# Hybrid Mamba-2 / RWKV-7 decoder layer on one Trainium2 core: four edits in the recurrent stage

## The chip, the cores and the metric

One Trainium2 chip, one of its eight cores. The metric is the device time of one execution of the program in microseconds (us). All arithmetic is on 32-bit floats. The median of three runs of the kernel before is 2946.23 us (2942.55 to 2946.69).

## The reference, cut to what matters

The program is one decoder layer for a prompt of 1024 tokens and 8 samples of 8 tokens each. It has an input projection, a Mamba-2 branch, an RWKV-7 branch, a merge, an output projection and a convolutional gated feed-forward block. The change touches the RWKV-7 branch alone, whose core is this recurrence for 16 heads of 64 channels, with a normalisation of `kk` before it and a group norm after it:

```python
def _rwkv7_scan(r, decay, k, v, kk, a, S0):
    def step(S, inp):
        r_t, w_t, k_t, v_t, kk_t, a_t = inp
        sa = jnp.einsum('bhvk,bhk->bhv', S, -kk_t)
        S = (S * w_t[:, :, None, :] + sa[..., None] * (kk_t * a_t)[:, :, None, :]
             + v_t[..., None] * k_t[:, :, None, :])
        return S, jnp.einsum('bhvk,bhk->bhv', S, r_t)
...
    kk = kk / jnp.maximum(jnp.sqrt(jnp.sum(kk * kk, axis=-1, keepdims=True)), 1e-12)
...
    mu = jnp.mean(yb, axis=-1, keepdims=True)
    var = jnp.mean((yb - mu) ** 2, axis=-1, keepdims=True)
...
    yb = yb + jnp.sum(r4 * k4 * lp['rwkv_r_k'].astype(f32), axis=-1, keepdims=True) * v4
```

## The kernel before, in words

Activations stand as channels (partitions) by tokens; the 1088 tokens are cut into three token groups of 384, 384 and 320 columns, the last of which ends in the 64 sample tokens. Every large product takes three passes on TensorE: weights and activations are each split into a rounded part (`hi`) and the rest (`lo`), and `mm3` (lines 253 to 257) issues hi by hi, hi by rest and rest by hi. `run_dense` (line 259) runs through the weight tiles; these are called the dense matmuls here. After every second step of `mm3` it calls `bg.step()`, which advances the background work of the stage by one piece.

In the recurrent stage, which is the first third of the span, that background is RWKV-7. Heads go in 8 pairs `p`, token groups `tg` in 3, and each job (p, tg) passes four lanes of Python generators:

- `rw_prep` (line 486): gates, decays, the normalisation, and then the pairwise products of the tokens within a unit of 64 tokens (`pair`, line 571). These are 64x64-tile matmuls, 16 for four units, into two PSUM tiles of the pool with tag `t`; a VectorE multiplication with a mask empties each tile into `tt` (line 581).
- `rw_inv` (line 601): inverse of a triangular matrix per unit, by 32x32-tile matmuls (lines 703, 728, 744), and transposes (lines 638, 738).
- `rw_scan` (line 752): the recurrence over 4 or 6 units. A unit is a chain: matmul at line 771, `rh` on VectorE (773), matmul 775, two copies of one half each of `pc` into `sav`, one on VectorE (776) and one on ScalarE (777), matmul 779, new state on VectorE (781). There are 128 units. For samples the same two copies stand at lines 822 and 823, before the matmul at 827, and the new sample states are four products at line 845 (`quarters`, line 830): two head halves `hf` by two groups `b` of four samples. Half `hf` writes the PSUM partitions from 64 x `hf`.
- `rw_post` (line 865): group norm and gate.

Sums over the 64 channels of a head are `colsum` (line 404): the operand is split by `halves` (line 397) into `xh`, which ScalarE casts, and `xl`, the rest, which VectorE computes from `xh`; then two accumulating matmuls, first with `xh` (line 405), then with `xl` (line 406). `pst()` gives PSUM tiles of tag `t`, of which there are two.

The order of the instructions on each engine is not the order of the Python code: when the program has been recorded, a list scheduler with its own cost estimates places every instruction in its engine's queue as its operands become ready by these estimates. `small` (line 241) keeps a batch of small matmuls in order by queueing each behind the one before (`issue_after`), and can add one more dependency to the first of them (`wait`). The engines then run their queues in order, and wait wherever the real time is later than the estimate.

Of the kernel before, what the change touches and what calls it, by code (L numbers as in the profile page):

```python
# [12 lines left out]
AF = mybir.ActivationFunctionType  # L13
# [91 lines left out]
def tile_hybrid_step(  # L105
# [380 lines left out]
    def rw_prep(p, tg):  # L486
# [32 lines left out]
        S.activation(rn[:, :n], ps[:, :n], AF.Ln, bias=tiny)  # L519
# [46 lines left out]
        evacs = None  # L566
        for u in range(0, nu, 4):
# [10 lines left out]
            small([lambda j=j, c0=c0, hf=hf: pair(j, c0, hf) for j in range(m) for c0, hf in ((0, 1), (64, 0), (64, 1), (0, 0))], wait=evacs)  # L578
            msk = tms if (tg == 2 and u == 4) else tm
            for hf in range(2):  # L580
                evacs = V.tensor_tensor(  # L581
                    out=tt[:, u:u + m, hf::2, :], in0=pa[hf][:, :m].rearrange("p u (x c) -> p u x c", x=2),
                    in1=msk.rearrange("p (x c) -> p x c", x=2).unsqueeze(1).to_broadcast([128, m, 2, 64]), op=ALU.mult,
                ).ins
# [9 lines left out]
        V.tensor_tensor(out=bv[:, :n], in0=ps[:, :n], in1=vv[:, :n], op=ALU.mult)  # L594
# [6 lines left out]
    def rw_inv(p, tg):  # L601
# [108 lines left out]
        S.copy(re[:, :nu], p3)  # L710
        S.copy(rv[:, :nu], pvw)
# [5 lines left out]
        V.tensor_tensor(out=zc[:, :nu], in0=zc[:, :nu], in1=p3, op=ALU.add)  # L717
# [29 lines left out]
        for hf in range(2):  # L747
            r0 = 64 * hf
            V.tensor_copy(tt[r0:r0 + 32, :nu, hf, 32:64], p3[r0:r0 + 32])
        jobs[p, tg] = (ar, tt, sav, bkt, wend, rv)  # L750

    def rw_scan(p, tg):
# [14 lines left out]
        for u in range(npu):  # L767
# [9 lines left out]
            S.copy(sav[64:128, u, 1, :], pc[64:128, 1, 64:128])  # L777
# [17 lines left out]
        if tg == 2:  # L795
# [27 lines left out]
            S.copy(sav[64:128, u, 1, :], pc[64:128, 1, :])  # L823
# [6 lines left out]
            quarters = [(hf, b) for hf in range(2) for b in (0, 4)]  # L830
# [31 lines left out]
        S.copy(yt[:, :n], ps[:, :n])  # L862
        lanes["post"].add(rw_post(p, tg, yt), lambda: (p, tg) in bonus)

    def rw_post(p, tg, yt):
# [7 lines left out]
        S.activation(sq[:, :n], ps[:, :n], AF.Ln, bias=geps, scale=1.0 / 64.0)  # L873
# [8 lines left out]
        V.scalar_tensor_tensor(out=yt[:, :n], in0=yt[:, :n], scalar=pv("lnb", p), in1=ps[:, :n], op0=ALU.add, op1=ALU.mult)  # L882
# [823 lines left out]
```

## Time and profile before

| | |
|---|---|
| median of 3 runs | 2946.23 us |
| profiled execution | 2947.11 us, span 2945.2 us |
| PE busy over the span | 2834.9 us, 96% |
| DVE busy | 1878.3 us, 64% |
| ACT busy | 1365.3 us, 46% |
| mean granted TensorE clock | 0.988 |
| recurrent stage, matmuls of `rw_post` as its last | ends at about 1058 us |

PE is TensorE with its matmuls, PEld its weight loads, DVE VectorE, ACT ScalarE, POOL GpSimd. A matmul of fp32 operands shows as two instructions in the trace; one of the dense matmuls as one. The ends of matmuls are modelled, and a matmul that streams shows as some 0.31 to 0.34 us though the next begins 0.15 to 0.17 us after it: so the starts tell the pace, and idle time before a matmul is counted only from the modelled end of the one before.

### The profile page before, as it was taken

What the parts mean: (1) busy time and instruction counts of PE and PEld (TensorE: products, weight loads), DVE (VectorE), ACT (ScalarE), POOL (GpSimd) and SP (SyncE); (2) the same over time, 40 slices, a digit from 0 to 9 for tenths busy, and PEclk for the clock granted to TensorE, in tenths of its full rate; (3) what the DMA queues carried; (4) which work ended last, traced back from release to release, by engine and by line L of the source; (5) the groups of instructions that cost most, each with busy time, mean ns of one, the idle gap of its engine ahead of it and who ended that gap; (6) DMA issues with size and microseconds to landing.
All of it is one profiled execution on the core that took longest, in us unless ns stands there. A gap on an engine that the chain in (4) does not pass through costs nothing.

```text
span 2945.2 us, 57204 instructions
## 1 busy us (share of the span) xinstructions
PE 2834.9 (96%) x22822; PEld 2631.3 (89%) x22822; DVE 1878.3 (64%) x4097; ACT 1365.3 (46%) x3108; POOL 698.6 (24%) x890
## 2 busy tenths in 40 slices
PE   8999999999999999999999989999999999999998
PEld 7887888888878899888888889999999999999998
DVE  6788777787788755878787753544264444444435
ACT  6666556555566655666666641222242222222223
POOL 3112212122121133555554421542220000000001
PEclk9999999999999999999999999999999999999999
DMA  3111111111111232343434564432211111111112
GB/s 113 37 36 43 42 39 51 35 47 41 45 37 41 69 86 66 115 139 111 141 108 148 150 216 128 149 110 85 83 54 51 58 51 51 51 52 57 51 51 86
DMA packets 160355, 229.86 MB, mean 78 GB/s; under 512 B 20940, under 2 KB 124632, under 8 KB 160088
## 3 DMA queue, kind: packets, MB, share of 16 engines
q1 hardware_dynamic: 160088, 226.20, 24.3%
q8 instruction: 180, 2.95, 0.4%
q14 instruction: 87, 0.71, 0.1%
HBM read 177.89 MB, written 48.26 MB: 77 GB/s over the span
## 4 chain that ended last, share of the span: by engine, by line
PE 46%; DVE 8%; ACT 4%; DMA 2%; issue 2%; POOL 1%; DVEq 0%; SPq 0%; ACTq 0%; POOLq 0%
PE psd L255 14%; PE psd L256 14%; PE psd L257 14%; DVE acc L1050 2%; DVE sg L1137 1%; DVE wlo L238 1%; DMA ld<-ya_d 1%; DVE sg L1127 1%; DVE yj L1234 1%; PE py L1180 1%; DMA ld<-yb_d 1%; DVE yj L1237 1%; PE py L1217 1%; PE py L1181 0%; PE ph L1183 0%
## 5 line engine op out<-in xcount | busy, mean ns | idle before, releaser
L255 PE MATMUL psd<-act,whi 128*128 128x384 f32 (+1 forms) x4344 | 1474.5, 339 | 14.7 <-ACT act L215 5.2
L257 PE MATMUL psd<-act,wlo 128*128 128x384 f32 (+1 forms) x4344 | 1435.0, 330 | 4.7 <-DVE wlo L238 4.7
L256 PE MATMUL psd<-act,whi 128*128 128x384 f32 (+1 forms) x4344 | 1434.2, 330 | 4.3 <-DVE act L216 4.0
L255 PEld LDWEIGHTS psd<-act,whi 128*128 128x128 f32 x4344 | 822.6, 189 | 43.9 <-issue 19.3
L256 PEld LDWEIGHTS psd<-act,whi 128*128 128x128 f32 x4344 | 822.3, 189 | 22.1 <-issue 10.0
L257 PEld LDWEIGHTS psd<-act,wlo 128*128 128x128 f32 x4344 | 822.0, 189 | 7.9 <-DVE wlo L238 5.3
L237 ACT CAST whi<-wraw 128x512 fp32r<-128x512 f32 x382 | 226.6, 619 | 499.3 <-PE psd L256 491.4
L238 DVE TENSOR_TENSOR wlo<-wraw,whi 128x512 fp32r<-128x512 f32 x382 | 289.0, 780 | 260.7 <-ACT whi L237 255.0
L1442 DVE TENSOR_TENSOR macc<-macc,psd 128x384 f32<-128x384 f32 (+1 forms) x216 | 114.6, 531 | 74.2 <-PE psd L257 73.8
L1399 POOL COPY fpo<-fraw 128x2 f32<-128x2 f32 x22 | 9.5, 430 | 613.1 <-ACT fraw L1397 613.1
L1050 DVE SCALAR_TENSOR_TENSOR acc<-craw,par,acc 128x1112 f32<-128x1112 f32 x72 | 116.3, 1615 | 5.5 <-ACT acc L1047 4.8
L1138 POOL TENSOR_TENSOR csb<-csb,cc 128x512 f32<-128x512 f32 (+1 forms) x72 | 98.5, 1374 | 77.4 <-ACT dec L1136 64.0
L1394 ACT COPY fraw<-psd 128x384 f32<-128x384 f32 x44 | 21.1, 479 | 133.2 <-PE psd L257 133.2
L1304 POOL TENSOR_TENSOR ld<-ld,rw 128x384 f32<-128x384 f32 (+1 forms) x48 | 54.3, 1152 | 114.7 <-DMA ld<-ya_d 111.0
L1326 POOL TENSOR_TENSOR macc<-macc,gt 128x384 f32<-128x384 f32 (+1 forms) x48 | 53.6, 1118 | 107.1 <-DVE gt L1325 107.1
L546 POOL TENSOR_TENSOR ar<-rm,wq 128x384 f32<-128x384 f32 (+1 forms) x24 | 20.8, 867 | 237.9 <-ACT wq L524 221.1
L1325 DVE TENSOR_TENSOR gt<-psd,gt 128x384 f32<-128x384 f32 (+1 forms) x48 | 25.5, 533 | 77.9 <-PE psd L257 70.7
L713 POOL MEMSET tt<- 64x384 f32 (+1 forms) x48 | 18.1, 377 | 240.6 <-PE pst L697 239.1
L1137 DVE TENSOR_TENSOR sg<-sg,cbm 128x512 f32<-128x512 f32 (+1 forms) x72 | 73.5, 1045 | 0.6
L613 ACT COPY uc<-tt 32x192 f32<-32x192 f32 (+1 forms) x96 | 49.4, 515 | 52.5 <-DVE tt L581 51.3
L627 POOL TENSOR_TENSOR bk<-bk,wend 128x768 f32<-128x768 f32 (+1 forms) x24 | 34.2, 1426 | 140.7 <-PE pst L573 104.8
L779 PE MATMUL pc<-sav,bkt 128*128 128x128 f32 x256 | 59.3, 314 | 8.3 <-ACT sav L777 7.0
(405 smaller groups left out, 4360.8 us busy)
## 6 DMA issues: line engine op xcount, KB each, us to landing
wraw<-in_wts SPq DMA_DIRECT2D x191, 512.0 KB, 3.2
csb<-cs_d SPq DMA_DIRECT2D x64, 256.0 KB, 4.2
gt<-g_d SPq DMA_DIRECT2D x48, 192.0 KB, 2.3
zt<-z_d SPq DMA_DIRECT2D x32, 256.0 KB, 4.6
z_d<-ge SPq DMA_DIRECT2D x32, 192.0 KB, 1.9
ya_d<-yj SPq DMA_DIRECT2D x8, 768.0 KB, 4.4
ld<-ya_d SPq DMA_DIRECT2D x32, 192.0 KB, 3.2
g_d<-ge SPq DMA_DIRECT2D x28, 192.0 KB, 1.9
```

What stands on the lines that cost most here:

```text
L237: S.copy(hi[:, c:c + 512], t[:, c:c + 512])
L238: V.tensor_tensor(out=lo[:, c:c + 512], in0=t[:, c:c + 512], in1=hi[:, c:c + 512].bitcast(F32), op=ALU.subtract)
L255: PE.matmul(ps, a, act[:, 0, :n], start=first, stop=False)
L256: PE.matmul(ps, a, act[:, 1, :n], start=False, stop=False)
L257: PE.matmul(ps, b, act[:, 0, :n], start=False, stop=last)
L779: last = PE.matmul(pc[:, 2, :], bkt[:, u, :], sav[:, u, :, :].rearrange("p h c -> p (h c)"), start=True, stop=True).ins
L1050: V.scalar_tensor_tensor(out=acc, in0=raw[:, j:j + L], scalar=cw(j), in1=acc, op0=ALU.mult, op1=ALU.add)
L1137: V.tensor_tensor(out=sg[0:m, :, :m], in0=sg[0:m, :, :m], in1=cbm[0:m, :m].unsqueeze(1).to_broadcast([m, 4, m]), op=ALU.mult)
L1138: G.tensor_tensor(out=ec[:, :, :m], in0=ec[:, :, :m], in1=cx[:, q0:q0 + m].unsqueeze(1).to_broadcast([128, 4, m]), op=ALU.mult)
L1304: G.tensor_tensor(out=t[:, :n], in0=t[:, :n], in1=scales[k // 4, tg][:, :n], op=ALU.mult)
L1326: G.tensor_tensor(out=macc[m][tg][:, :n], in0=macc[m][tg][:, :n], in1=gt[:, :n], op=ALU.add)
L1442: V.tensor_tensor(out=x1[m][tg][:, :n], in0=x1[m][tg][:, :n], in1=ps[:, :n], op=ALU.add)
```

## The change

It makes four edits, all in the code of the recurrent stage.

1. `colsum` multiplies the rest first and the rounded part second.
2. `quarters` goes through the halves first and through the sample groups second, so that the two products that stand together write different halves of the PSUM partitions.
3. The second copy into `sav`, for units and for samples, moves from ScalarE to VectorE.
4. Instructions that empty a PSUM tile of tag `t` are noted in a list (`read`). The first matmul of each batch of pairwise products now depends on the last two of the list, the readers of both PSUM tiles that the batch takes over. Before, only a second batch had one such dependency, on the last mask multiplication.

```diff
+    readers = []
+
+    def read(ins):
+
+        readers.append(ins.ins)
+
-    def small(calls, behind=None, wait=None):
+    def small(calls, behind=None, wait=()):
...
-            if wait is not None:
-                tc.add_manual_dep(behind, wait.name, mybir.DependencyInfo(mybir.DependencyClass.Sync, mybir.DependencyReason.DATA), reason="small")
-                wait = None
+            for ins in wait:
+                tc.add_manual_dep(behind, ins.name, mybir.DependencyInfo(mybir.DependencyClass.Sync, mybir.DependencyReason.DATA), reason="small")
+            wait = ()
...
     def colsum(ps, m, parts_, n):
-        PE.matmul(ps[:, :n], m, parts_[0][:, :n], start=True, stop=False)
-        PE.matmul(ps[:, :n], m, parts_[1][:, :n], start=False, stop=True)
+        PE.matmul(ps[:, :n], m, parts_[1][:, :n], start=True, stop=False)
+        PE.matmul(ps[:, :n], m, parts_[0][:, :n], start=False, stop=True)
...
-        S.activation(sg[:, :n], ps[:, :n], AF.Exp, scale=-1.0, bias=nw0[:, p:p + 1])
+        read(S.activation(sg[:, :n], ps[:, :n], AF.Exp, scale=-1.0, bias=nw0[:, p:p + 1]))
...
-            small([lambda j=j, c0=c0, hf=hf: pair(j, c0, hf) for j in range(m) for c0, hf in ((0, 1), (64, 0), (64, 1), (0, 0))], wait=evacs)
+            small([lambda j=j, c0=c0, hf=hf: pair(j, c0, hf) for j in range(m) for c0, hf in ((0, 1), (64, 0), (64, 1), (0, 0))], wait=readers[-2:])
...
             V.tensor_copy(sav[0:64, u, 0, :], pc[0:64, 1, 0:64])
-            S.copy(sav[64:128, u, 1, :], pc[64:128, 1, 64:128])
+            V.tensor_copy(sav[64:128, u, 1, :], pc[64:128, 1, 64:128])
...
             V.tensor_copy(sav[0:64, u, 0, :], pc[0:64, 1, :])
-            S.copy(sav[64:128, u, 1, :], pc[64:128, 1, :])
+            V.tensor_copy(sav[64:128, u, 1, :], pc[64:128, 1, :])
...
-            quarters = [(hf, b) for hf in range(2) for b in (0, 4)]
+            quarters = [(hf, b) for b in (0, 4) for hf in range(2)]
```

`read(...)` is put around the other readers of `t` tiles in the same way. New lines shift the numbers: what is line 405, 573, 775, 776, 777, 779 before is 411, 578, 783, 784, 785, 787 after, and the dense 255, 256, 257 are 261, 262, 263.

Since the scheduler works the order out anew, much of the stage's order moves. Three places show how. The first is PE's queue in the first head pair, at a batch of pairwise products for four units (`pst<-ar_129,bk`, 16 matmuls). Before:

```order
L703 MATMUL pst<-vt,um 32x32 x24
L573 MATMUL pst<-ar_129,bk 64x128
L256 MATMUL psd<-act_340,whi 128x384
L257 MATMUL psd<-act_340,wlo 128x384
L255 MATMUL psd<-act_352,whi 128x384
L573 MATMUL pst<-ar_129,bk 64x128 x15
L256 MATMUL psd<-act_352,whi 128x384
L257 MATMUL psd<-act_352,wlo 128x384
```

Of the change:

```order
L709 MATMUL pst<-vt,um 32x32 x24
L262 MATMUL psd<-act_340,whi 128x384
L263 MATMUL psd<-act_340,wlo 128x384
L261 MATMUL psd<-act_352,whi 128x384
L262 MATMUL psd<-act_352,whi 128x384
L578 MATMUL pst<-ar_129,bk 64x128 x16
L263 MATMUL psd<-act_352,wlo 128x384
L261 MATMUL psd<-act_359,whi 128x384
```

The first product, which stood alone three dense matmuls ahead of the other 15, now stands with them. Over the stage the 544 pairwise products stand in 57 pieces where they stood in 83, and the runs of dense matmuls are broken 510 times where they were broken 548 times.

The second place is PE's queue in the fifth head pair, from a unit's matmul at line 775 on, across a column sum (`pst<-xh,conr` and `pst<-xl,conr`) and three transposes. Before:

```order
L775 MATMUL pc<-rh,tt 128x128
L255 MATMUL psd<-act_333,whi 128x384
L405 MATMUL pst<-xh,conr 128x320
L638 MATMUL pst<-con,vm 128x128 x3
L256 MATMUL psd<-act_333,whi 128x384
L257 MATMUL psd<-act_333,wlo 128x384
L406 MATMUL pst<-xl,conr 128x320
```

Of the change:

```order
L783 MATMUL pc<-rh,tt 128x128
L261 MATMUL psd<-act_333,whi 128x384
L262 MATMUL psd<-act_333,whi 128x384
L263 MATMUL psd<-act_333,wlo 128x384
L261 MATMUL psd<-act_340,whi 128x384
L411 MATMUL pst<-xl,conr 128x320
L412 MATMUL pst<-xh,conr 128x320
L643 MATMUL pst<-con,vm 128x128 x3
L262 MATMUL psd<-act_340,whi 128x384
L263 MATMUL psd<-act_340,wlo 128x384
L787 MATMUL pc<-sav,bkt 128x128
```

The sum's two matmuls now stand together, three dense matmuls later than the first of them stood, and ahead of the transposes. Of the 96 column sums 46 stood together before; all 96 do now.

The third place is DVE's queue at the same point: `rh`, the copies into `sav`, and the new state `st` of a unit. Before:

```order
L401 TENSOR_TENSOR xl<-rn,xh 128x384
L773 TENSOR_TENSOR rh<-pc,rv 128x128
L594 TENSOR_TENSOR bv<-pst,vm 128x384
L776 COPY sav<-pc 64x64
L420 SCALAR_TENSOR_TENSOR rm<-carry,par,rm 128x1
L418 SCALAR_TENSOR_TENSOR rm<-psd,par,rm 128x383
L516 SCALAR_TENSOR_TENSOR c<-rreset,sg 128x320
L781 SCALAR_TENSOR_TENSOR st<-st,wend,pc 128x128
```

Of the change:

```order
L781 TENSOR_TENSOR rh<-pc,rv 128x128
L599 TENSOR_TENSOR bv<-pst,vm 128x384
L696 STREAM_TRANSPOSE zt<-vt 128x192
L407 TENSOR_TENSOR xl<-rn,xh 128x320
L784 COPY sav<-pc 64x64
L785 COPY sav<-pc 64x64
L426 SCALAR_TENSOR_TENSOR rm<-carry,par,rm 128x1
L424 SCALAR_TENSOR_TENSOR rm<-psd,par,rm 128x383
L522 SCALAR_TENSOR_TENSOR c<-rreset,sg 128x320
L486 TENSOR_TENSOR llo<-lwa,lwh 64x128
L789 SCALAR_TENSOR_TENSOR st<-st,wend,pc 128x128
```

The unit's two copies now follow each other on DVE, here behind a transpose and a rest `xl` that stood elsewhere; in 108 of the 128 units nothing stands between the two. From the end of the stage on, the order of PE, DVE and ACT is the same in both programs.

## Rows read from the trace of the kernel before

**Rows 1.** The page, part 1: busy us (share of the span) xinstructions.

```profile
PE 2834.9 (96%) x22822; PEld 2631.3 (89%) x22822; DVE 1878.3 (64%) x4097; ACT 1365.3 (46%) x3108; POOL 698.6 (24%) x890
```

**Rows 2.** Windows, recurrent stage: us, busy (xinstructions) of PE, PEld, DVE, ACT, POOL, PEclk, DMA.

```profile
60.00:1030.00 970.00, 925.90 (x10442) 792.31 (x10441) 756.03 (x2260) 595.27 (x1517) 173.44 (x321) 1.00 0.13 43
```

**Rows 3.** Waits of PE, 70 to 1030 us: us in total, times, longest us.

```profile
PE pc L779 <- ACT sav L777: 7.0, 15, 1.2
PE pst L405 <- ACT xh L400: 5.8, 7, 1.0
PE pst L573 <- DVE tt L581: 3.9, 7, 1.3
PE py L827 <- ACT sav L823: 3.6, 5, 0.8
PE pst L703 <- DVE zt L690: 3.3, 2, 2.2
PE pc L775 <- DVE rh L773: 3.3, 8, 0.9
PE pst L703 <- DVE sav L776: 3.0, 5, 0.6
```

**Rows 4.** Waits of PE's weight loads, 70 to 1060 us.

```profile
PEld pc L779 <- ACT sav L777: 24.1, 60, 1.5
...
PEld pst L405 <- ACT xh L400: 13.1, 23, 1.3
...
PEld pc L775 <- DVE rh L773: 12.3, 32, 1.2
...
PEld py L827 <- ACT sav L823: 5.3, 6, 1.1
```

**Rows 5.** Line 777: duration ns min/median/max; what its engine sat idle for (us, times).

```profile
L777 ACT COPY sav<-pc x128: 207/207/209, 135.9 to 1049.1; 64x64 f32<-64x64 f32 x128
...
  DVE sav L776: 49.0, 41
```

**Rows 6.** Timeline, one unit's copies: start us, us, engine, what xcount [idle before].

```profile
398.97 0.22 DVE L776 COPY sav<-pc 64x64 f32<-64x64 f32 x1 [0.23 <-PE pc L775]
...
400.06 0.21 ACT L777 COPY sav<-pc 64x64 f32<-64x64 f32 x1
...
400.32 0.49 PE L779 MATMUL pc<-sav,bkt 128*128 128x128 f32 x2 [0.51 <-ACT sav L777]
```

**Rows 7.** Timeline of PE at two of the four sample products.

```profile
241.31 1.08 PE L845 MATMUL pn<-sx,bkt 128*64 128x256 f32 x4
```

**Rows 8.** Timeline of PE in the next stage, products that alternate halves.

```profile
1163.59 0.45 PE L1180 MATMUL py<-sg,xdt 128*64 128x128 f32 x4
```

**Rows 9.** Timeline of PE into and out of small matmuls, and across a column sum.

```profile
500.85 0.34 PE L406 MATMUL pst<-xl,conr 128*128 128x384 f32 x1
501.03 0.33 PE L256 MATMUL psd<-act,whi 128*128 128x384 f32 x1
501.20 0.34 PE L257 MATMUL psd<-act,wlo 128*128 128x384 f32 x1
...
507.21 0.31 PE L257 MATMUL psd<-act,wlo 128*128 128x320 f32 x1
507.45 0.62 PE L703 MATMUL pst<-vt,um 32*32 32x32 f32 x48
...
508.24 0.39 PE L255 MATMUL psd<-act,whi 128*128 128x320 f32 x1
508.47 0.30 PE L256 MATMUL psd<-act,whi 128*128 128x320 f32 x1
508.62 0.31 PE L257 MATMUL psd<-act,wlo 128*128 128x320 f32 x1
```

**Rows 10.** Groups by line and shape: busy us, mean ns of one.

```profile
L1180 PE MATMUL py<-sg,xdt 128*64 128x128 f32 x512 | 58.7, 292 | 0.8 <-DVE sg L1137 0.8
...
L845 PE MATMUL pn<-sx,bkt 128*64 128x256 f32 x64 | 17.5, 393 | 0.5 <-POOL sx L836 0.5
```

More of the change, by code (lines that the diff above doesn't have):

```diff
@@ L518, in rw_prep @@
         colsum(ps, onesbd_r, halves(rn, n), n)
-        S.activation(rn[:, :n], ps[:, :n], AF.Ln, bias=tiny)
+        read(S.activation(rn[:, :n], ps[:, :n], AF.Ln, bias=tiny))
         S.activation(rn[:, :n], rn[:, :n], AF.Exp, scale=-0.5)
@@ L564, in rw_prep @@
         tt = rt([128, 6, 4, 64], "tt", 3)
-        evacs = None
         for u in range(0, nu, 4):
@@ L576, in pair @@
                 )
[L578 removed]
+            small([lambda j=j, c0=c0, hf=hf: pair(j, c0, hf) for j in range(m) for c0, hf in ((0, 1), (64, 0), (64, 1), (0, 0))], wait=readers[-2:])
             msk = tms if (tg == 2 and u == 4) else tm
             for hf in range(2):
[L581 removed]
+                read(V.tensor_tensor(
                     out=tt[:, u:u + m, hf::2, :], in0=pa[hf][:, :m].rearrange("p u (x c) -> p u x c", x=2),
                     in1=msk.rearrange("p (x c) -> p x c", x=2).unsqueeze(1).to_broadcast([128, m, 2, 64]), op=ALU.mult,
[L584 removed]
+                ))
             if u + m < nu:
@@ L593, in rw_prep @@
         colsum(ps, onesbd_r, halves(rn, n), n)
-        V.tensor_tensor(out=bv[:, :n], in0=ps[:, :n], in1=vv[:, :n], op=ALU.mult)
+        read(V.tensor_tensor(out=bv[:, :n], in0=ps[:, :n], in1=vv[:, :n], op=ALU.mult))
         bonus[p, tg] = bv
@@ L646, in rw_inv @@
             S.copy(sav[64:128, units_, 0, :], pvw[rows, :m, 0, :])
-            S.copy(sav[0:64, units_, 1, :], pvw[rows, :m, 1, :])
+            last = S.copy(sav[0:64, units_, 1, :], pvw[rows, :m, 1, :])
+        read(last)
         pd = rt([128, 512], "pd")
@@ L709, in rw_inv @@
         re = um
-        S.copy(re[:, :nu], p3)
-        S.copy(rv[:, :nu], pvw)
+        read(S.copy(re[:, :nu], p3))
+        read(S.copy(rv[:, :nu], pvw))
         for hf in range(2):
@@ L716, in rw_inv @@
         small(tiles32(p3, re, zc))
-        V.tensor_tensor(out=zc[:, :nu], in0=zc[:, :nu], in1=p3, op=ALU.add)
+        read(V.tensor_tensor(out=zc[:, :nu], in0=zc[:, :nu], in1=p3, op=ALU.add))
         V.transpose(out=zt[:, :nu].rearrange("p u c -> p (u c)"), in_=zc[:, :nu].rearrange("p u c -> p (u c)"))
@@ L732, in rw_inv @@
             r0 = 64 * hf
-            S.copy(re[r0 + 32:r0 + 64, :nu], p3[r0 + 32:r0 + 64])
+            last = S.copy(re[r0 + 32:r0 + 64, :nu], p3[r0 + 32:r0 + 64])
+        read(last)
         for u in range(0, nu, 4):
@@ L738, in rw_inv @@
                 PE.transpose(ps[:, 128 * j:128 * j + 128], bk[:, u + j, :], ident)
-            S.copy(bkt[:, u:u + m, :], ps[:, :128 * m].rearrange("p (u c) -> p u c", c=128))
+            read(S.copy(bkt[:, u:u + m, :], ps[:, :128 * m].rearrange("p (u c) -> p u c", c=128)))
         yield
@@ L748, in rw_inv @@
             r0 = 64 * hf
-            V.tensor_copy(tt[r0:r0 + 32, :nu, hf, 32:64], p3[r0:r0 + 32])
+            last = V.tensor_copy(tt[r0:r0 + 32, :nu, hf, 32:64], p3[r0:r0 + 32])
+        read(last)
         jobs[p, tg] = (ar, tt, sav, bkt, wend, rv)
@@ L861, in rw_scan @@
         colsum(ps, cen_r, parts_, n)
-        S.copy(yt[:, :n], ps[:, :n])
+        read(S.copy(yt[:, :n], ps[:, :n]))
         lanes["post"].add(rw_post(p, tg, yt), lambda: (p, tg) in bonus)
@@ L872, in rw_post @@
         colsum(ps, onesbd_r, halves(sq, n), n)
-        S.activation(sq[:, :n], ps[:, :n], AF.Ln, bias=geps, scale=1.0 / 64.0)
+        read(S.activation(sq[:, :n], ps[:, :n], AF.Ln, bias=geps, scale=1.0 / 64.0))
         S.activation(sq[:, :n], sq[:, :n], AF.Exp, scale=-0.5)
@@ L881, in rw_post @@
             load_lora("gup", gupw, p + 1)
-        V.scalar_tensor_tensor(out=yt[:, :n], in0=yt[:, :n], scalar=pv("lnb", p), in1=ps[:, :n], op0=ALU.add, op1=ALU.mult)
+        read(V.scalar_tensor_tensor(out=yt[:, :n], in0=yt[:, :n], scalar=pv("lnb", p), in1=ps[:, :n], op0=ALU.add, op1=ALU.mult))
         store(yb_d[p][:, t0:t0 + n], yt[:, :n])
```

2 lines of the change are left out of this document (1 added, 1 removed).

## The prediction

> **What bounds the kernel now.** The page's busy times come first [rows 1]. TensorE is busy for 96% of the span, so time can be won in two ways: fewer matmul slots on PE, or less of the 4% in which it stands still. The order of the program is the same from the end of the recurrent stage on, so only that stage can change. Its window is next [rows 2]: of 970.0 us PE is busy for 925.9 us, which leaves 44.1 us idle. DVE is busy for 756.0 us, 78%, and ACT for 595.3 us, 61%. The granted clock is 1.00 there, the full 2.4 GHz, so no term below is a matter of the clock.
>
> Then the waits of PE [rows 3], which say for whom it stood still: line 779 for the copy on ACT (7.0 us), the column sums for ACT's cast (5.8), the pairwise products for the mask on DVE (3.9), the sample product 827 for ACT (3.6), and others. This view sees a stall only from the modelled end of the matmul before. The waits of the weight loads [rows 4] see it from the other side, too early: line 779 is held there for 24.1 us in 60 units of 128. The true stall is between the two.
>
> **The change part by part.** The sum is made against the profiled execution, 2947.1 us (span 2945.2 and 1.9 us around it), which is 0.9 us above the median of the runs shown.
>
> *Sample products in pairs.* Two products, four instructions, take 1.08 us to their end [rows 7], and one takes 393 ns [rows 10]; so three follow the first at (1080 - 393)/3 = 229 ns each, one after another. All write 64 of the 128 columns. The next stage has products of the same form, 64 columns wide, that alternate the halves: four instructions in 0.45 us with one at 292 ns [rows 8, 10], which leaves 158 ns for three followers, or 53 ns each. At the pace of the 256-column ones a follower of 128 columns would take 229 x 128/256 = 115 ns, twice as much. So halves run beside each other there. The paired products should lose two of three followers' slots, 0.46 us a pair. There are two pairs in each of 8 head pairs, 16 in all: -7.3 us at most, and nothing if they do not overlap. I take -7, since rows 8 are of the same shape.
>
> *Both copies on VectorE.* Now the ACT copy takes 207 ns [rows 5], but it begins only after the DVE copy of the same PSUM tile has ended: ACT sat idle for that in 41 units, 49.0 us in all [rows 5]. Elsewhere it comes later still, behind ACT's other work: in rows 6 DVE ends at 399.19, ACT begins at 400.06, and PE stands still for 0.51 us. Two copies on DVE would have ended at about 399.41. After the change line 779 (787) waits for DVE alone, as line 775 does for `rh`: that wait is 3.3 us on PE and 12.3 us on the weight loads [rows 3, 4], and I take it as what remains. The gain is 7.0 - 3.3 = 3.7 us by the one view and 24.1 - 12.3 = 11.8 us by the other; I take -8, the middle. The sample copy before line 827 is waited for 3.6 us by the one view and 5.3 us by the other; there are 8 of them against 128 units, so 8/128 of the same waits remain, 0.2 and 0.8 us: -3.4 to -4.5, I take -3.5. Together -11.5, bounds -7 and -16.
>
> Here a rule speaks against the change. The Trainium skill (TensorEngine Tiling (Array Packing), section PSUM Bottleneck) advises to use both ScalarE and VectorE to empty PSUM. By that rule the copies would cost VectorE time that ScalarE had to spare, at worst 136 x 0.22 = +30 us in place of -11.5, and the sum would be +21; the rows show that in this chain the two engines take turns on one tile, so that the split saves nothing here, and the term stays.
>
> *Batches queued whole.* A break in the dense matmuls has a price on entry and on exit: 507.21 to 507.45 is 0.24 us and 508.24 to 508.47 is 0.23, where 508.47 to 508.62 is 0.15 [rows 9]; together 0.17 us. A column sum between dense matmuls has none: 500.85 to 501.03 and 501.03 to 501.20 are 0.18 and 0.17 [rows 9]. The order has 38 fewer breaks in all, 26 fewer pieces of pairwise products: 26 x 0.17 = -4.4 us, bounds 0 and 38 x 0.17 = -6.5. That the first matmul of a batch now waits for both readers costs nothing of itself: the 3.9 us for the mask [rows 3] are waited at the first instead of the second matmul, and dense matmuls stand ahead of it.
>
> *Column sums.* The pair now begins when `xl` is there, one DVE operation after `xh`. It also stands later in the queue, by three dense matmuls (0.5 us) in the place shown ahead. So the 5.8 us [rows 3] that the first matmul waited for ACT's cast should come back as a wait for `xl`: 0. The bounds are -5.8, all of it gone, and +5.8, as much again: half of what the weight loads wait there, 13.1 us [rows 4], is not seen by PE's own view.
>
> *What it gives back.* DVE takes on 136 copies of 0.22 us [rows 6], 30 us, and goes from 78% to 81% of the stage. PE's waits for DVE are 3.9 + 3.3 + 3.3 + 3.0 = 13.5 us [rows 3]. If they grow as DVE's idle share shrinks, 22/19, that is +2.1; I take +3, bounds 0 and a doubling, +13.5. ACT loses 136 x 0.21 = 28 us; nobody waits for it longer. GpSimd's masks, SP's queue and the DMAs keep their number.
>
> Sum: -7 - 11.5 - 4.5 + 0 + 3 = **-20 us**: 2927 for a profiled execution, and 2946 - 20 = **2926 us** for the median. With all bounds at their best (-7.3 - 16 - 6.5 - 5.8 + 0) it is -36, or 2910.
>
> **The rivals.**
>
> *VectorE's queue takes over (slower).* The whole chain of a unit, `rh`, both copies and the new state, would now stand in one queue, among rests, masks and scans. Each copy that comes late holds line 787, the state behind it, and through DVE's order everything that stands behind the copies. For it: 78% busy already, and in the third place of the order shown the copies went behind a transpose and an `xl`. Against it: its waits are 13.5 us of 44 today, and the chain has dense work between its links. It decides once those waits grow by more than the 23 us won elsewhere and the 6 us of a measurement, to just over three times 13.5; at 3.4 times (+32) the time is 2946 - 23 + 32 = 2955 us. The rule on sharing PSUM work, cited above from the Trainium skill, points this way; by the rows it has this chance and no more. Chance 8%.
>
> *The stalls only move.* The order is made from estimates, and PE is held where a producer is later than estimated. A stall removed at line 787 is then waited out at the next small matmul, whose producer has not become faster: ACT's cast, the mask, `zt`. What is left are the paired products, given back in part by DVE: 2946 +- 6, say 2942. For it: the stalls have several producers [rows 3], of which the change removes one. Against it: 10.6 us of them hang on the ACT copy alone. Chance 16%.
>
> *The stalls are larger than PE's view shows.* If the weight loads' view is the true one, and the whole batches also keep their matmuls side by side, the sum comes to its best bounds, 2910 us. Chance 17%.
>
> *The pairs do not overlap* (edit 2 does nothing): the sum without its -7, 2933 us. Chance 8%.
>
> **How the numbers follow.** The forecast itself, 2914 to 2938, has 51%. Faster by more than 0.2% (5.9 us, about what a measurement of this kernel can tell from no change): 51 + 17 + 8 = 76%. Within it: 16%. Slower: 8%. The range that should hold 8 in 10 is 2906 to 2942 us: it goes a few us past the best bounds, since the ones taken from a single view may be short, takes in the pairs that do not overlap, and reaches the edge of no change; it leaves out the slow rival and the upper half of the second.
>
> **What would show it.** Right: in the recurrent stage PE's waits for the copies of `sav` fall from 7.0 and 3.6 to about 3 and under 1 us, and name DVE; four instructions of line 853 end in some 0.62 us instead of 1.08; pieces of the pairwise products of a single matmul become rare in the timeline; PE's busy time in the stage falls by about 10 us and its idle time by as much again. Wrong: PE's waits for DVE add up to 30 us or more, or line 853 still shows 1.08, or the last matmul of `rw_post` does not start some 20 us before its 1058 us. The stages behind it should take what they took; if they move by more than 3 us, something is at work that I have not seen.

## The result and the profile after

The changed kernel takes 2962.97 us (median of 6 runs, 2950.56 to 2966.86) against 2943.11 us before in the same session (6 runs, 2939.15 to 2946.69): a ratio of 1.0061 [1.0041, 1.0081]. It is slower by 18 us where 20 us less was forecast, and lies above the range. Its profiled execution took 2959.31 us (span 2957.4 us, mean granted clock 0.983); that of before took 2947.11 us at 0.988.

The page's busy times and the window of the recurrent stage, which answer to [rows 1] and [rows 2]:

```profile
PE 2827.7 (96%) x22822; PEld 2638.2 (89%) x22822; DVE 1921.8 (65%) x4233; ACT 1335.3 (45%) x2972; POOL 699.6 (24%) x890
```

```profile
60.00:1030.00 970.00, 908.86 (x10333) 788.47 (x10331) 793.13 (x2374) 561.22 (x1374) 171.34 (x321) 0.98 0.13 43
```

VectorE took over the 136 copies and stands at 82% of the window where it stood at 78%. PE did 109 instructions fewer in the same 970 us, stood still for 61.1 us of them where it was 44.1, and the granted clock is no longer 1.00. The waits of PE between 70 and 1060 us, which answer to [rows 3]:

```profile
PE pst L411 <- DVE xl L407: 14.0, 30, 0.9
PE pst L578 <- DVE tt L586: 10.0, 9, 1.5
PE pc L779 <- DVE st L789: 9.8, 20, 1.0
PE pst L709 <- DVE zt L696: 5.5, 8, 2.2
PE pc L783 <- DVE rh L781: 3.8, 8, 1.3
PE pn L853 <- POOL sx L844: 3.5, 2, 2.4
PE pc L787 <- DVE sav L785: 3.5, 2, 2.2
```

The wait for the second copy (7.0 us, line 779 before, 787 now) fell to 3.5 us, and the 3.6 us of the sample copy are gone from the list. But the column sum waits for `xl` 14.0 us where it waited for `xh` 5.8 us, the mask 10.0 us where it was 3.9, and the matmul that takes the state `st` (line 771 before, 779 now) 9.8 us where it was 1.1. `xl`, the mask and `st` are all made on VectorE: the waits shown here for it add up to 46.6 us, where those of before came to 13.5 (with the small rows that are not shown, 49.4 and 16.4).

**Where the time went.** The first matmul of a head pair's scan that takes `rh`, in the first, second, seventh and eighth head pair, and the last `rw_post` matmul (timeline of PE; start us, us), before:

```profile
133.86 0.38 PE L775 MATMUL pc<-rh,tt 128*128 128x128 f32 x2
251.47 0.49 PE L775 MATMUL pc<-rh,tt 128*128 128x128 f32 x2 [0.86 <-DVE rh L773]
855.51 0.49 PE L775 MATMUL pc<-rh,tt 128*128 128x128 f32 x2
966.56 0.49 PE L775 MATMUL pc<-rh,tt 128*128 128x128 f32 x2 [0.69 <-DVE rh L773]
1057.98 0.70 PE L879 MATMUL pst<-gact,gup 128*128 128x320 f32 x2
```

And after:

```profile
136.38 0.38 PE L783 MATMUL pc<-rh,tt 128*128 128x128 f32 x2
259.48 0.49 PE L783 MATMUL pc<-rh,tt 128*128 128x128 f32 x2 [0.55 <-DVE rh L781]
857.35 0.49 PE L783 MATMUL pc<-rh,tt 128*128 128x128 f32 x2 [1.32 <-DVE rh L781]
978.67 0.38 PE L783 MATMUL pc<-rh,tt 128*128 128x128 f32 x2
1071.88 0.70 PE L887 MATMUL pst<-gact,gup 128*128 128x320 f32 x2
```

From the second to the seventh head pair the change gains: 597.87 us instead of 604.04, or 1.2 us a pair. It loses at both ends: 2.5 us up to the first of these rows, 5.5 from there to the second, 10.3 between the seventh and the eighth, and 1.8 behind. At the end of the stage it is 13.9 us late. What follows takes 1885.5 us of the span, where it took 1887.2.

The windows of the two ends, and one between, show how (us; busy and instructions of PE, PEld, DVE, ACT, POOL; PEclk; DMA). After:

```profile
120.70:124.10 3.40, 1.22 (x8) 0.92 (x7) 3.31 (x9) 2.04 (x6) 0.15 (x2) 1.00 0.16 58
124.10:127.50 3.40, 3.39 (x121) 3.15 (x122) 2.87 (x7) 1.67 (x6) 0.82 (x2) 0.50 0.17 55
151.40:154.80 3.40, 1.74 (x65) 1.40 (x65) 3.28 (x10) 1.32 (x4) 0.11 (x1) 1.00 0.00 0
154.80:158.20 3.40, 3.40 (x75) 3.13 (x69) 3.29 (x12) 1.64 (x6) 0.82 (x2) 0.50 0.09 24
229.90:233.30 3.40, 2.37 (x95) 2.05 (x92) 3.33 (x9) 2.21 (x6) 0.98 (x4) 1.00 0.16 53
233.30:240.10 6.80, 6.80 (x61) 5.89 (x63) 2.75 (x6) 3.48 (x10) 1.24 (x2) 0.50 0.01 2
281.10:284.50 3.40, 1.97 (x16) 1.21 (x14) 3.20 (x6) 0.00 (x0) 0.64 (x2) 1.00 0.07 19
284.50:287.90 3.40, 3.40 (x13) 3.40 (x13) 1.29 (x5) 2.49 (x6) 2.36 (x5) 0.50 0.46 154
943.30:946.70 3.40, 1.20 (x8) 0.88 (x6) 3.34 (x9) 0.39 (x1) 0.00 (x0) 1.00 0.00 0
946.70:956.90 10.20, 9.95 (x193) 8.55 (x195) 6.45 (x16) 4.15 (x12) 2.17 (x6) 0.50 0.12 33
963.80:967.20 3.40, 1.56 (x9) 1.00 (x8) 1.83 (x5) 2.88 (x6) 3.07 (x6) 1.00 0.00 0
967.20:974.00 6.80, 6.26 (x18) 5.05 (x19) 3.86 (x20) 1.55 (x3) 2.46 (x4) 0.50 0.08 29
```

Six stretches, 34.1 us together before rounding, ran at 0.50, which is 1.2 of 2.4 GHz. The profile of before has none between 40 us and the end of the stage. In each stretch ahead of a fall PE stood still for a good part (1.20 to 2.37 us busy of 3.40). In five of the six VectorE was full (3.20 to 3.34 of 3.40). Ahead of the sixth, at 963.8 us, it was not (1.83): there GpSimd had 3.07 us, and PE waited 2.38 us for the mask `sx` of the sample products, which GpSimd makes behind other work of its own. Half of 34.1, 17 us, is what the six stretches cost at most, since at half rate the same work takes twice as long. They lie where the time was lost: 13.6 us of them between 124 and 241 us, 17.0 behind 946 us.

One of the stalls close up, 943 to 947 us. PE's timeline:

```profile
944.05 0.34 PE L263 MATMUL psd<-act,wlo 128*128 128x384 f32 x1
946.59 0.71 PE L787 MATMUL pc<-sav,bkt 128*128 128x128 f32 x2 [2.20 <-DVE sav L785]
```

And VectorE's, some rows of it, without idle time:

```profile
940.14 0.23 DVE L784 COPY sav<-pc 64x64 f32<-64x64 f32 x1
...
945.05 0.61 DVE L546 SCALAR_TENSOR_TENSOR rn<-rm,par,c 128x384 f32<-128x384 f32 x1
945.58 0.70 DVE L689 STREAM_TRANSPOSE pd<-ub 128x512 f32<-128x512 f32 x1
946.31 0.23 DVE L785 COPY sav<-pc 64x64 f32<-64x64 f32 x1
```

The copy that line 787 waits for takes 0.23 us and begins 6.2 us after the first copy of the same unit: between the two stand the end of the inverse and the gates of the next job. On ScalarE, where it used to be, none of these stood ahead of it; the same unit's second copy began at 936.48 us there, 0.5 us after its first, and PE did not wait for it.

### The profile page after: what moved, and what is told of

Read it like the earlier page. It is cut to its first block, busy times and chain, and to the rows that moved or that the text cites. A ratio compares the mean times of both kernels' runs of the same rounds, so it can differ in the third digit from the quotient of the medians.

```text
span 2957.4 us, 57246 instructions
## 1 busy us (share of the span) xinstructions
PE 2827.7 (96%) x22822; PEld 2638.2 (89%) x22822; DVE 1921.8 (65%) x4233; ACT 1335.3 (45%) x2972; POOL 699.6 (24%) x890
## 4 chain that ended last, share of the span: by engine, by line
PE 44%; DVE 8%; ACT 4%; issue 2%; DMA 2%; POOL 1%; DVEq 0%; SPq 0%; POOLq 0%; ACTq 0%
PE psd L261 14%; PE psd L263 14%; PE psd L262 14%; DVE acc L1058 2%; DVE sg L1145 1%; DVE sg L1135 1%; DVE wlo L238 1%; DVE yj L1242 1%; DMA ld<-ya_d 1%; DMA ld<-yb_d 1%; DVE yj L1245 1%; PE py L1225 0%; PE py L1188 0%; POOL ld L1312 0%; ACT sg L1138 0%
## 5 line engine op out<-in xcount | busy, mean ns | idle before, releaser
L261 PE MATMUL psd<-act,whi 128*128 128x384 f32 (+1 forms) x4344 | 1474.4, 339 | 15.7 <-ACT act L215 5.2
L261 PEld LDWEIGHTS psd<-act,whi 128*128 128x128 f32 x4344 | 824.8, 190 | 44.1 <-issue 18.4
L552 POOL TENSOR_TENSOR ar<-rm,wq 128x384 f32<-128x384 f32 (+1 forms) x24 | 22.8, 950 | 223.8 <-ACT wq L530 196.5
L779 PE MATMUL pc<-st,ar 128*128 128x128 f32 x256 | 56.4, 302 | 10.1 <-DVE st L789 9.8
```

The source lines that it names most:

```text
L261: PE.matmul(ps, a, act[:, 0, :n], start=first, stop=False)
L779: PE.matmul(pc[:, 0, :], ar[:, u, 0:2, :].rearrange("p h c -> p (h c)"), st, start=True, stop=True)
```

## The experiments

Each was timed in five rounds beside the kernel before. A ratio and its interval stand at each; "half clock" is the time at a granted clock of 0.50 between 40 us and the end of the stage in its one profile.

### One edit alone, and one left out

Edit 1 alone (`colsum` begins with the rest):

```diff
-        PE.matmul(ps[:, :n], m, parts_[0][:, :n], start=True, stop=False)
-        PE.matmul(ps[:, :n], m, parts_[1][:, :n], start=False, stop=True)
+        PE.matmul(ps[:, :n], m, parts_[1][:, :n], start=True, stop=False)
+        PE.matmul(ps[:, :n], m, parts_[0][:, :n], start=False, stop=True)
```

> Edit 1 alone: the rest first in each column sum. Theory A: within 4 us of before, since the wait for ACT's cast only comes back as one for xl. Theory B: slower by 6 us or more, and PE's waits for xl stand near 14 us in this kernel alone.

Edit 2 alone:

```diff
-            quarters = [(hf, b) for hf in range(2) for b in (0, 4)]
+            quarters = [(hf, b) for b in (0, 4) for hf in range(2)]
```

> Edit 2 alone: sample products paired across halves. Both theories: four instructions of the sample products end in 0.6 to 0.7 us instead of 1.08, and the kernel is 5 to 7 us faster. If halves do not run beside each other the group still takes 1.08 us and the time is that of before.

Edit 3 alone:

```diff
-            S.copy(sav[64:128, u, 1, :], pc[64:128, 1, 64:128])
+            V.tensor_copy(sav[64:128, u, 1, :], pc[64:128, 1, 64:128])
...
-            S.copy(sav[64:128, u, 1, :], pc[64:128, 1, :])
+            V.tensor_copy(sav[64:128, u, 1, :], pc[64:128, 1, :])
```

> Edit 3 alone: both copies into sav on VectorE, the rest as before. Theory A (VectorE's queue): the copies lengthen a queue that is already full in places; PE then stands still for single stretches of over 1 us, and the granted clock of the recurrent stage falls to 1.2 GHz behind them. It expects this kernel slower than before by 8 to 20 us, with a clock of the recurrent stage (60 to 1040 us) below 0.99. Theory B (the column sums: PE now waits for the rest xl, 14.0 us): edit 3 alone removes ACT's copy and gains, so 5 to 12 us faster, with the clock at 1.00.

Edits 1, 2 and 4, the change without edit 3:

```diff
-            V.tensor_copy(sav[64:128, u, 1, :], pc[64:128, 1, 64:128])
+            S.copy(sav[64:128, u, 1, :], pc[64:128, 1, 64:128])
...
-            V.tensor_copy(sav[64:128, u, 1, :], pc[64:128, 1, :])
+            S.copy(sav[64:128, u, 1, :], pc[64:128, 1, :])
```

> Edits 1, 2 and 4, with the second copy left on ScalarE. Theory A: the stage's clock stays at 1.00, and the kernel is faster than before by 6 to 14 us. Theory B: it keeps the wait for xl and so is no faster than before, within 4 us or slower.

Edit 4 alone (the list of readers, and nothing else of the change):

```diff
-            small([lambda j=j, c0=c0, hf=hf: pair(j, c0, hf) for j in range(m) for c0, hf in ((0, 1), (64, 0), (64, 1), (0, 0))], wait=evacs)
+            small([lambda j=j, c0=c0, hf=hf: pair(j, c0, hf) for j in range(m) for c0, hf in ((0, 1), (64, 0), (64, 1), (0, 0))], wait=readers[-2:])
```

> Edit 4 alone: the first matmul of each pairwise batch depends on both readers. Theory W (the whole batches are what lowers the clock): a mean clock of about 0.984 and 8 to 12 us slower than before, as all edits but the copies were. Theory D (VectorE is full in stretches, each edit shifts PE ahead of it, and only the sum of them makes stalls long enough for the clock to fall): within 6 us of before, clock 0.987 to 0.989.

Edits 1, 2 and 3 (the same lines the other way round, from the change):

> Edits 1, 2 and 3. Theory W: clock as before, 0.988, and within 4 us of before. Theory D: slower than before by 4 us or more, with single stalls of PE of over 1 us on VectorE in the stage and half-clock stretches behind them.

Edits 2, 3 and 4, the sums as before:

> Edits 2, 3 and 4. Theory S (the rest first is what does the harm: it puts one more VectorE operation ahead of each column sum, and every combination with it was slow): within 5 us of before, clock of the whole 0.987 or more. Theory V (VectorE's queue alone, from edit 3): 8 us or more slower, clock 0.985 or less.

Edits 1, 3 and 4, the `quarters` as before:

> Edits 1, 3 and 4. Theory S and theory V both: 10 to 18 us slower than before, clock 0.980 to 0.985. If it is within 5 us of before, the pairs, by bringing PE to VectorE's full stretch earlier, are what makes the long stalls.

Measured:

| kernel | us | ratio to before | half clock, us |
|---|---|---|---|
| edit 1 alone | 2951.59 | 1.0019 [1.0010, 1.0028] | 6.8 |
| edit 2 alone | 2949.95 | 1.0013 [1.0004, 1.0022] | 3.4 |
| edit 3 alone | 2947.98 | 1.0015 [1.0006, 1.0024] | 0 |
| edit 4 alone | 2944.57 | 0.9994 [0.9985, 1.0002] | 3.4 |
| all but 1 | 2952.85 | 1.0025 [1.0013, 1.0036] | 30.7 |
| all but 2 | 2953.95 | 1.0025 [1.0014, 1.0037] | 37.5 |
| all but 3 | 2956.68 | 1.0045 [1.0032, 1.0057] | 23.9 |
| all but 4 | 2957.43 | 1.0039 [1.0025, 1.0053] | 17.1 |
| all four | 2962.97 | 1.0061 [1.0041, 1.0081] | 34.1 |

No edit is the culprit by itself, and none wins alone. Three of them cost 0.13 to 0.19% each, edit 4 nothing that can be told from zero, and each is worth 0.16 to 0.36% less harm when left out of the four. So the theories that lay the loss on the copies, on the sums, or on edit 4 and the clock fall as single causes: without any one of them the kernel is still slower, by 0.25% or more in the median. What the four may have in common, as a reading, is that PE comes sooner, or with a different operand, to something that VectorE makes. Two of the single edits miss both of their theories. In edit 1 alone PE's wait for `xl` is 5.1 us and not 14, about the 5.8 us for `xh` that it takes the place of, and the kernel loses 5.8 us all the same. Edit 3 alone keeps a clock of 1.00 in the stage and is neither 8 to 20 us slower nor faster. The profiles of a kernel are single executions (edit 3's, at 2942.11 us, lies 6 us below its median), so the last column shows where the loss can sit rather than how large it is.

The edit that failed most plainly is the one whose mechanism was surest. Edit 2 alone, timeline of PE at one pair of sample products and at the first `rh` of the next scan:

```profile
492.54 0.65 PE L845 MATMUL pn<-sx,bkt 128*64 128x256 f32 x4
497.00 0.49 PE L775 MATMUL pc<-rh,tt 128*128 128x128 f32 x2 [0.96 <-DVE rh L773]
```

The four instructions take 0.65 us instead of 1.08, so the halves run beside each other. But the `rh` that comes next is now waited for 0.96 us where the same place before had 0.21:

```profile
494.84 0.49 PE L775 MATMUL pc<-rh,tt 128*128 128x128 f32 x2 [0.21 <-DVE rh L773]
```

Its maker, in the VectorE timeline of before:

```profile
494.24 0.35 DVE L681 TENSOR_SCALAR ub<-zl,con 128x256 f32<-128x256 f32 x1
494.50 0.29 DVE L773 TENSOR_TENSOR rh<-pc,rv 128x128 f32<-128x128 f32 x1
```

`rh` stands in VectorE's queue behind the end of the inverse (line 681 above), and VectorE is full there, in the kernel before already (its windows):

```profile
485.00:490.00 5.00, 5.00 (x29) 4.26 (x29) 4.93 (x24) 2.31 (x5) 1.18 (x2) 1.00 0.11 41
490.00:495.00 5.00, 4.79 (x26) 3.67 (x25) 5.00 (x11) 1.86 (x5) 0.00 (x0) 1.00 0.42 141
```

Two pairs of products save 0.86 us in a head pair and 0.75 comes back at `rh`: in this stretch PE waits out most of what it saves. That makes the middle of the stage level with before (603.87 us from the second to the seventh head pair, where before has 604.04). It does not make a loss: what this kernel loses in the stage lies at the two ends, 2.2 us up to the first `rh` and 2.1 between the seventh head pair and the eighth.

### VectorE relieved by leaving work out

The next kernels test whether VectorE is what takes the gain back: they leave out four VectorE operations of `rw_inv` (lines 670 to 679: the two 512-column products and two reductions that couple the 8x8 blocks of the inverse). This part of the computation is not done in them. The edit against the kernel before:

```diff
-        V.tensor_tensor(
-            out=p4, in0=vt[:, 8:16, 0:8].rearrange("p k i -> p i k").unsqueeze(2).to_broadcast([128, 8, 8, 8]),
...
-        V.tensor_reduce(out=zl[:, 8:16, 0:8].rearrange("p j i -> p i j"), in_=p4, op=ALU.add, axis=mybir.AxisListType.X)
```

> The kernel before without the four VectorE operations that couple the two 8x8 blocks of the inverse (two products and two sums of 512 elements, lines 670 to 679), which leaves that part of the computation out: some 3.5 us less of VectorE in each of 24 jobs. Theory D: PE's waits for rh behind them go and the kernel is 5 to 20 us faster than before. Were VectorE not the limit there, no change within 3 us.

The same with edit 2 (its line as above):

> The same omission with edit 2 (paired sample products). Theory D: with VectorE relieved the pairs give their 0.86 us per head pair, so 5 to 7 us faster than the omission alone, where edit 2 alone gave nothing. Rival (the pairs' gain is lost to something else, as the order of the queue): no difference from the omission alone, within 3 us.

The same with all four edits:

> All four edits, with the four VectorE operations that couple the 8x8 blocks of the inverse left out, as in the earlier omission. Theory D (VectorE's full stretches take back what the edits save, and the long stalls there lower the clock): with VectorE relieved the edits give most of what was forecast, 10 to 20 us faster than the omission without the edits (2939.5), with a clock of 0.987 or more. Rival (the edits' harm is in their own new waits, for the rest xl and the second copy): slower than the omission without the edits, by 5 us or more.

| work left out, and | us | ratio to before | the edits' part |
|---|---|---|---|
| no edit | 2939.50 | 0.9975 [0.9966, 0.9984] | |
| edit 2 | 2934.09 | 0.9958 [0.9944, 0.9973] | -5.4 us (alone, with the work in: +4.2) |
| all four | 2926.78 | 0.9936 [0.9924, 0.9949] | -12.7 us, or some -11.5 by the ratios (with the work in: +18) |

The last run decides most. With some 3.5 us of VectorE work less per job (two products of 1.06 and 1.04 us and two reductions of 0.69), of which there are 24, the same edits gain. Where the gain turns into a loss is seen from 40 us to the end of the stage (columns as in the windows above). Before, then changed:

```profile
40.00:1058.68 1018.68, 973.98 (x10811) 835.12 (x10811) 778.97 (x2311) 616.34 (x1567) 181.37 (x330) 1.00 0.13 43
40.00:1072.58 1032.58, 971.29 (x10820) 844.64 (x10819) 823.07 (x2449) 586.52 (x1432) 179.40 (x330) 0.98 0.13 42
```

The work left out, without the edits, then with all four:

```profile
40.00:1049.20 1009.20, 969.94 (x10816) 831.76 (x10816) 713.01 (x2217) 619.52 (x1567) 182.98 (x330) 1.00 0.13 43
40.00:1040.30 1000.30, 950.83 (x10820) 825.92 (x10819) 753.71 (x2351) 586.37 (x1433) 180.04 (x330) 1.00 0.13 44
```

| the edits' effect on the stage, us | PE busy | PE idle | end of the stage |
|---|---|---|---|
| work in | -2.7 | +16.6 | +13.9 |
| work left out | -19.1 | +10.2 | -8.9 |

The edits add idle time either way. With the work in it is 6.4 us more; the larger difference, 16.4 us, stands in PE's busy time, and it is about half of the 34.1 us at half clock, of which the kernel with the work left out and all four edits has none (with edit 2 only it has 10.2). So of the 22.8 us between the gain and the loss some 16 are the clock and some 6 longer waits, as far as one profile of each can tell. The head pairs in the middle do not decide it: from the second to the seventh the edits gain 6.2 us with the work in and 8.2 with it left out.

PE's waits for VectorE stay on the list of the kernel that gains:

```profile
PE pst L578 <- DVE tt L586: 11.0, 10, 1.5
...
PE pst L697 <- DVE zt L684: 2.2, 2, 1.6
```

Over all rows they come to 42.9 us there and to 49.4 in the changed kernel, so their sum is not the loss. What is missing are the longest: 1.6 us at most, where the changed kernel has 2.2 for VectorE and 2.4 for GpSimd.

One thing the omission does not separate. The four operations are load for VectorE and also links of the inverse's chain, and without them the order is worked out anew: where the work is left out and no edit made, VectorE is still full in the inverse, but earlier, and the `rh` of the same head pair comes 5 us and more behind it.

```profile
475.00:480.00 5.00, 5.00 (x36) 4.62 (x35) 4.93 (x30) 2.21 (x6) 2.81 (x5) 1.00 0.02 5
```

```profile
488.58 0.29 DVE L761 TENSOR_TENSOR rh<-pc,rv 128x128 f32<-128x128 f32 x1 [1.08 <-PE pc L759]
```

That these operations turn the edits' gain into a loss is shown; whether by their load, by the length of their chain or by their place in the order is not.

### VectorE relieved by other engines

All of these start from edits 2 and 4, which alone give 2944.89 us, 0.9998 [0.9989, 1.0007], no change:

> Edits 2 and 4. Theory D: the pairs' gain is waited back at rh also here, so the time is that of edit 4 alone, 1 to 4 us faster than before. Rival: the two gains add, 6 to 9 us faster.

The two 512-column products of the inverse on GpSimd:

```diff
-        V.tensor_tensor(
+        G.tensor_tensor(
...
-        V.tensor_tensor(
+        G.tensor_tensor(
```

> Edits 2 and 4 with the two products of 512 elements in the inverse (1.08 and 1.04 us on VectorE, lines 670 and 675) moved to GpSimd, which is idle there. If VectorE's full stretch is what takes the pairs' gain: 6 to 14 us faster than before, clock 0.988. If the chain of the inverse is the limit and not VectorE's load: no faster than before, since a product takes longer on GpSimd.

Two products of `rw_prep` on GpSimd:

```diff
-        V.tensor_tensor(out=q[:, :n], in0=q[:, :n], in1=kx[:, :n], op=ALU.mult)
+        G.tensor_tensor(out=q[:, :n], in0=q[:, :n], in1=kx[:, :n], op=ALU.mult)
...
-        V.tensor_tensor(out=a[:, :n], in0=a[:, :n], in1=kk[:, :n], op=ALU.mult)
+        G.tensor_tensor(out=a[:, :n], in0=a[:, :n], in1=kk[:, :n], op=ALU.mult)
```

> Edits 2 and 4 with two multiplications of rw_prep (lines 534 and 539, some 0.45 us each, 24 jobs) moved to GpSimd. They lie outside the full stretch behind the inverse. If what counts is VectorE's load in that stretch, the pairs' gain stays lost there: 0 to 5 us faster than before. If the mean load counts, as much faster as with the products of the inverse moved, 6 to 14 us.

Both copies into `sav` on ScalarE:

```diff
-            V.tensor_copy(sav[0:64, u, 0, :], pc[0:64, 1, 0:64])
+            S.copy(sav[0:64, u, 0, :], pc[0:64, 1, 0:64])
...
-            V.tensor_copy(sav[0:64, u, 0, :], pc[0:64, 1, :])
+            S.copy(sav[0:64, u, 0, :], pc[0:64, 1, :])
```

> Edits 2 and 4 with both copies into sav on ScalarE, the other way round from edit 3. VectorE loses 136 copies of 0.22 us. Theory D: PE's waits for rh shrink and the kernel is 4 to 10 us faster than before. If ScalarE's own queue (a copy behind activations of 0.5 us) is what PE waits for: PE's waits for sav on ScalarE rise from 7 us to over 15, and it is no faster than before.

The two scalings behind the inverse on ScalarE:

```diff
-        V.tensor_scalar(out=ub[:, :, 0:16], in0=zl, scalar1=cv("par0"), scalar2=None, op0=ALU.mult)
-        V.tensor_scalar(out=ub[:, :, 16:32], in0=zl, scalar1=cv("par1"), scalar2=None, op0=ALU.mult)
+        S.activation(ub[:, :, 0:16], zl, AF.Identity, scale=cv("par0"))
+        S.activation(ub[:, :, 16:32], zl, AF.Identity, scale=cv("par1"))
```

> Edits 2 and 4 with the two scalings at the end of the full stretch (0.35 us each, lines 680 and 681, just ahead of rh in VectorE's queue) on ScalarE. Theory D: the wait for rh behind them shrinks by some 0.7 us per head pair, 5 to 9 us faster than before. If a link to another engine in that chain costs more than the load it takes off, as it did on GpSimd: slower than before, by 10 us or more.

VectorE's busy time is taken from 40 us to the end of the stage; edits 2 and 4 alone have 778.8 us there.

| moved | us | ratio to before | VectorE busy, us |
|---|---|---|---|
| inverse's products to GpSimd | 2987.41 | 1.0142 [1.0127, 1.0157] | 765.7 |
| `rw_prep`'s products to GpSimd | 2997.12 | 1.0173 [1.0157, 1.0189] | 785.7 |
| both copies to ScalarE | 2948.80 | 1.0011 [1.0002, 1.0020] | 766.8 |
| scalings to ScalarE | 2952.81 | 1.0024 [1.0015, 1.0032] | 775.8 |

All four were to take load off VectorE, and all four lose, where the theory of VectorE's full stretch had expected gains. They relieved it of little: 3 to 13 us, and the second of nothing, where the work left out was worth 66 (713.0 instead of 779.0). So they do not test what a relieved VectorE would give. With both copies on ScalarE PE's wait for them is 4.0 us, not over 15, and its wait for `rh` is 10.8 us where edits 2 and 4 alone have 5.1: neither theory had that. With the inverse's products on GpSimd, the sum behind the first of them waits on VectorE, and PE's largest wait is for `rh`, which stands in the same queue:

```profile
L680 DVE TENSOR_REDUCE ub<-pd 128x64 f32<-128x512 f32 x24 | 16.4, 685 | 29.7 <-POOL pd L676 29.7
```

```profile
PE pc L783 <- DVE rh L781: 20.5, 15, 3.1
```

A chain that goes to another engine and back puts a wait into VectorE's queue, and what stands behind it is late. That reading is argued from the waits; no run took it apart further. A second price stands in the timeline of the same kernel:

```profile
477.49 1.53 POOL L681 TENSOR_TENSOR pd<-zl,ub 128x512 f32<-128x512 f32 x1 [0.80 <-DVE ub L680]
```

```profile
477.52 1.91 DVE L544 SCALAR_TENSOR_TENSOR k<-rn,k 128x384 f32<-128x384 f32 x1
```

This VectorE operation takes 0.55 us as the median of those in this kernel that do not overlap a moved product, and 1.91 us here, where it begins with one. Over the run 7 of its 24 executions overlap one, with a median of 1.91 us. The operation at line 238 shows the same (1.06 us in 13 overlaps, 0.68 elsewhere), while `rh`, which reads a PSUM tile, does not (0.28 us either way). Of some 50 us of products moved, VectorE is therefore 13 us less busy. A `rw_prep` product takes 1222 ns in the mean on GpSimd, where the same line has a median of 541 ns on VectorE with edits 2 and 4:

```profile
L540 POOL TENSOR_TENSOR c<-c,km 128x384 f32<-128x384 f32 (+1 forms) x24 | 29.3, 1222 | 10.9 <-DVE c L539 10.9
```

No version with all the work in it beats the kernel before by an amount that can be told from nothing; edit 4 alone, at 0.9994 [0.9985, 1.0002], comes nearest.

## Why the prediction was wrong, step by step

**The step that failed is "what it gives back": +3 us, from VectorE's mean load.** It scaled PE's waits for VectorE with the engine's idle share of the whole stage (78% to 81%, 22/19). They went from 13.5 us to 46.6, +33, where even the bound was +13.5. Together the waiting terms of the sum (-11.5, 0 and +3) had 8.5 us less idle time; PE's idle time in the stage grew by 16.6 us. VectorE's load is not even: behind the inverse it stood at 4.93 and 5.00 of 5.00 us before the change, and in edit 2 alone 0.75 of 0.86 us saved was waited out behind that stretch. In the changed kernel five of the six long standstills fall where VectorE had 3.20 us or more of 3.40. With four of VectorE's operations left out per job the same edits gain 12.7 us. The window by stretches of 5 us, which shows the load, was not read.

**"No term below is a matter of the clock"** failed with it, and was the larger part. It is true of the trace before, and was taken as true of the change. The standstills of the changed kernel were followed by 34 us at half rate, up to 17 us lost; without them the stage would have ended at some 1055 us (1071.9 - 17) instead of 1058.0. The table of the stage, with the work in and left out, puts the clock at some 16 us by another way. A third way is the list of executions: the changed kernel took 2950.56 us at a mean clock of 0.987, 2959.31 at 0.983, 2962.61 at 0.982 and 2963.32 to 2966.86 at 0.980, and 13 executions of before at 0.987 have a median of 2947.86 us (2945.47 to 2951.13). At the same clock, then, the changed kernel is 2.7 us slower, from a single execution, and not 18. So the four edits as such, with the work in, come out near nothing, between 3 us gained and 3 lost, and the clock accounts for most of the loss. No run held the clock apart from the stalls, so the split is an estimate. The Trainium skill (Perfetto Trace Analysis, section Matmul Optimizations) says that the matmul engine scales its power with its use, so that matmuls should be issued back to back; the rows at 0.50 behind standstills agree, and the prediction did not weigh this rule.

**Sample products in pairs, -7.** The mechanism was right (four instructions in 0.65 us, 0.62 forecast), and the size only where the edit stands alone. Edit 2 by itself has 13 of 16 pairs at 0.65 us, 11.5 us in all where before had 18.1. In the changed kernel 7 of 16 are at 0.65 and the sum is 15.7: -2.4 us. Others are split by the operand mask `sx` on GpSimd, which comes late (timeline of PE, the third head pair's products and the seventh's):

```profile
490.90 1.22 PE L853 MATMUL pn<-sx,bkt 128*64 128x256 f32 x4
...
967.74 1.86 PE L853 MATMUL pn<-sx,bkt 128*64 128x256 f32 x4 [2.38 <-POOL sx L844]
```

In the first of these the second mask begins at 490.80 us and ends at 491.41, when the first product has long started, so its partner cannot run beside it; in the kernel before both masks were made by 484.60, ahead of products at 485.51. The second of these stands in a stretch at half clock. With edits 2 and 4, without the copies on VectorE, 12 pairs are at 0.65.

**Both copies on VectorE, -11.5.** Right about its own waits (7.0 to 3.5 us, 3.6 us gone) and wrong about the sum: `st` behind the copies took over 9.8 us (7.9 with edit 3 alone). The rule of the Trainium skill that was set against this term (TensorEngine Tiling (Array Packing), section PSUM Bottleneck: use both engines to empty PSUM) comes out right in its direction, though far from the +30 us worked out for it: edit 3 alone is 1.0015 [1.0006, 1.0024].

**Column sums, 0.** Right for the edit alone, past the bad bound in company: 5.8 us of waits for `xh` became 5.1 for `xl` with edit 1 alone and 14.0 with all four, +8.2 where the bound was +5.8. Edit 1 alone still costs 5.8 us (1.0019 [1.0010, 1.0028]), so its loss does not stand in this wait; PE's wait for ScalarE's copy went from 7.0 to 11.0 us there. What made it grow is open.

**Batches queued whole, -4.5.** The sign may hold. In the traces the pairwise products stand alone in 45 places before and in 7 after, as forecast; edit 4 alone has a head pair of 120.2 us in the middle of its profile where before has 121.7. Over its runs it gives 1.7 us, within the noise.

The slow rival, VectorE's queue, had 8% and named a copy that comes late in that queue, as at 946 us, and the sign by which it shows: PE's waits for VectorE past 3 times 13.5 us. Its 2955 us lacked the clock, and its sign alone does not decide: the kernel with the work left out and all four edits waits for VectorE 42.9 us and gains. The stages behind moved by 1.7 us, within the 3 us that were allowed.

## What to carry to other kernels

A stage's mean load is no measure for what an engine can still take: read the engine that is to receive work, and the engine that the bottleneck will wait for next, in windows of a few microseconds around the place of the change. Here VectorE, at 78% in the mean, was full for 5 to 10 us at a time; there a saving on the bottleneck was mostly waited back, and a copy of 0.23 us put into its queue held PE for 2.2. And a stall of PE is to be priced with the granted clock of what follows it: here, stretches of 3.4 to 10.2 us at half rate, which were most of the loss. Work moved to another engine relieves the full one only if its operations do not grow longer beside it: look at their durations after the move.

## What was not expected of the hardware

- A standstill of PE of 2.2 us, amid a stage that is 94% busy, was followed by 10.2 us at half rate (946.7 to 956.9 us). It does not always happen. Both kernels have a wait of 2.2 us for `zt` at about 122 us: in the changed one half clock followed, in the one before (the longest wait at line 703 in [rows 3]) it did not. Nor did it behind four waits of 1.54 us for the mask in the middle of the changed kernel's stage.
- VectorE's operation at line 544 took 1.91 us where it overlapped a product on GpSimd and 0.55 us elsewhere.
- Less busy time on an engine can go with more waiting for it: 765.7 us instead of 779.0 on VectorE in the stage, with 20.5 us of waits for `rh` instead of 3.3.
